# A two-layer decoder trunk on one core: the order of products around the chunk ends, side products placed later, and how zeros and stores are issued

## The chip, the core and the metric

One core of a Trainium2 chip runs the whole program in one launch. TensorE (PE in the profile) does the matrix products, VectorE (DVE), ScalarE (ACT) and GpSimd (POOL) the rest of the arithmetic, and SyncE (SP) issues almost all transfers between memory and the on-chip buffers. The metric is device microseconds of one execution, the median of several runs; less is better.

## The reference

512 tokens of width 1024, with 16 learned tokens put ahead of them, go through two layers. Each layer is a feed-forward half step, a token mixer and another feed-forward half step. Layer 0 mixes by chunked gated linear attention with 4 heads; layer 1 by sliding-window attention over one shared set of keys and values, which is made after layer 0. Each of the sub-layers has a norm ahead of it and one behind it. Cut to what matters:

```
def rmsnorm(x, g):
    return x * lax.rsqrt(jnp.mean(x * x, axis=-1, keepdims=True) + EPS) * g

def swiglu(x, w_in, w_out):
    gate, up = jnp.split(x @ w_in, 2, axis=-1)       # 1024 -> 2 x 2816
    return (jax.nn.silu(gate) * up) @ w_out          # 2816 -> 1024

h = jnp.concatenate([meta, x], axis=1)               # 16 + 512 tokens
for layer in range(2):
    g = norm_gains[layer]
    h = h + 0.5 * rmsnorm(swiglu(rmsnorm(h, g[0]), w_ffn_in[layer, 0], w_ffn_out[layer, 0]), g[1])
    hn = rmsnorm(h, g[2])
    mix = gla_mixer(hn, ...) if layer == 0 else swa_mixer(hn, ..., k_sh, v_sh)
    h = h + rmsnorm(mix, g[3])
    h = h + 0.5 * rmsnorm(swiglu(rmsnorm(h, g[4]), w_ffn_in[layer, 1], w_ffn_out[layer, 1]), g[5])
    if layer == 0:
        k_sh, v_sh = shared_kv(h, kv_norm, w_kv, cos, sin)
return h[:, 16:]
```

## The kernel before

**Layout.** Activations lie transposed: the width of 1024 is 8 tiles of 128 partitions, the tokens run along the free dimension. `H` is the residual stream, `Y` the output of a sub-layer before its norm. Tokens come in two groups, called gi 0 and gi 1: 272 and 256 in layer 0, 256 and 256 in layer 1 (the 16 added tokens are only needed as keys there). Every float32 operand is split into a high and a low half, each of the type fp32r: ACT copies the high half (L226, L245 for weights, L425 for inputs, L774 for hidden tiles), DVE subtracts to get the low half (L227, L246, L426, L775). A product is then three matmuls: high by high, low by high, high by low (`mm3s`, L333). All of them are issued by one helper, so nearly all have the line L162 in the profile, and are told apart by their tiles.

**A feed-forward block** (`ffn`, L604) goes over its 22 hidden tiles of 128 in four chunks of 4, 6, 6 and 6.

- The first chunk uses plain products. `x_first` (L509) computes several output tiles at once, in tiles named x, while the inputs of the norm are still being built one after another: all tiles for group 0, then all for group 1. A group of at most 256 tokens takes half a PSUM bank, so two outputs share one bank; each such bank is first written by a product of zeros, 512 wide (L532), and the products behind it only add. The same routine starts the two mixers and the shared keys and values (tiles x with inputs x_l0m, x_kv, x_l1m).
- The other chunks use seven products instead of eight for each 2 x 2 block (class `Strassen`, L711): `head`, `body` and `tail` issue the products 11, s1, s2, 12, s3, s4, 22 of 12 matmuls each into the banks a, c, d and e. ACT and DVE carry partial sums between the banks (L749 to L765). When the last product of a tile, "22" with the factor t4 in bank a, is done, a job called `gated` multiplies (L770, L771) and splits the hidden tile (L774, L775).
- After each chunk `out_proj` (L552) multiplies the chunk's hidden tiles by the output weights and adds the result into `Y` (tiles y). A *unit* is one output tile for one token group: three matmuls for each of the chunk's hidden tiles, the last hidden tile last. Layer 1 works 512 tokens wide there, but for the last chunk, which goes by the groups of 256.

**Norms.** Squares are added up on POOL and ACT (accumulators acc_...). A product with a matrix of ones (tiles st_...) sums over the partitions. `rstd` (L348) then computes an inverse square root with some eleven small instructions on POOL or DVE, puts it on a diagonal (dg_..., L383) and broadcasts it over the partitions by a second product (tiles r_...). `Operand.factors` (L436) does so ahead of a sub-layer, `Residual.run` (L453) behind one. The GLA mixer does it for each head (st_go, r_go).

**Order.** The order is made while the program is built. Side work is written as generators that give back a delay; `Flow` (L60) keeps a clock that moves on by an estimate for each matmul issued, and `flow.pump` between matmuls runs the jobs that are due. A wait of `flow.wait` runs jobs until the named ones are done, whatever the clock says. So the delays FACT (1.5), CHAIN (5) and STATE_KEYS (1.5) decide between which matmuls the st_, r_ and pk products stand. A scheduler then orders the instructions of each engine; an engine runs its own queue in order, and waits for other engines by semaphores.

**The end.** `Residual.store` (L471) scales `Y`, adds it to `H` and issues one transfer for each of the 8 tiles of 128 x 256 and each token group on SP, 16 in all (L482). For the second group the additions of tiles 0 to 3 are on POOL.

## Time and profile before

| | us |
|---|---|
| three runs | 1931.07, 1934.42, 1936.41 |
| median | 1934.42 |
| the profiled execution | 1931.38 |
| its span on the core | 1929.5 |

The mean granted clock of TensorE was 0.996 in the profiled execution. Rows of groups read: line, engine, operation, output tile and inputs, form, count; then busy time, mean ns of one, idle time of the engine just before them and what ended it. Rows of the timeline read: start, duration, engine, line, operation, output and inputs, form, count, and in brackets the idle time before and its releaser; a row with a count stands for several instructions in a row, and its duration runs to the end of the last.

### The profile page before, as it was taken

To read this page: it belongs to the slowest core of one execution; us is meant where nothing else is said; L and a number is where in the kernel's file an instruction comes from. 1 tells how busy PE (TensorE), PEld (TensorE's weight loads), DVE (VectorE), ACT (ScalarE), POOL (GpSimd) and SP (SyncE) were. 2 spreads that over 40 slices of the span, in tenths; PEclk is the share of its full clock that TensorE was granted. 3 is DMA by queue.
4 is the path that set the end of the run, shared out by engine and by line. 5 is a ranking of instruction groups with operands and counts; after the bars stand their busy time and mean duration, and the time that the engine had idled before them with its cause. 6 is when DMAs were issued, how large, how long until landed. Compare 5 with 4: busy or idle time off the path is not lost.

```text
span 1929.5 us, 37402 instructions
## 1 busy us (share of the span) xinstructions
PE 1888.9 (98%) x14522; PEld 1798.1 (93%) x14522; DVE 1420.1 (74%) x2868; ACT 1001.7 (52%) x2268; POOL 215.1 (11%) x417
## 2 busy tenths in 40 slices
PE   8999999999999999999999999999998999999997
PEld 7999999999999999999999898989976898989897
DVE  7885858676464788585887786868788779858584
ACT  5663636653245555353574453535645665636363
POOL 2000000321111400000033000000352140000002
PEclk9999999999999999999999999999999999999998
DMA  4332333322113123323351123233421212333331
GB/s 163 104 100 88 103 96 106 114 74 69 45 52 113 56 72 95 102 91 102 99 176 45 61 88 115 87 112 99 132 66 34 77 45 72 98 105 107 101 112 44
DMA packets 102144, 174.61 MB, mean 90 GB/s; under 512 B 11472, under 2 KB 24272, under 8 KB 101968
## 3 DMA queue, kind: packets, MB, share of 16 engines
q1 hardware_dynamic: 101680, 172.11, 28.2%
q8 instruction: 113, 1.85, 0.4%
q14 instruction: 63, 0.52, 0.1%
q10 hardware_dynamic: 288, 0.13, 0.0%
HBM read 170.10 MB, written 2.10 MB: 89 GB/s over the span
## 4 chain that ended last, share of the span: by engine, by line
PE 70%; DVE 19%; ACT 6%; issue 3%; POOL 1%; DMA 0%; SPq 0%; DVEq 0%; ACTq 0%; POOLq 0%
PE y L162 30%; PE x L162 16%; PE a L162 11%; DVE raw L251 5%; PE c L162 4%; DVE w_s L246 3%; DVE w L246 3%; ACT w_s L245 3%; PE d L162 2%; DVE w L227 2%; PE o L162 1%; ACT w L226 1%; PE po L162 1%; DVE hidl0f L775 1%; PE sc L162 0%
## 5 line engine op out<-in xcount | busy, mean ns | idle before, releaser
L246 DVE TENSOR_TENSOR w_s<-raw,w_s 128x512 fp32r<-128x512 f32 x288 | 194.0, 690 | 129.7 <-ACT w_s L245 127.6
L227 DVE TENSOR_TENSOR w<-raw,w 128x512 fp32r<-128x512 f32 x378 | 244.9, 673 | 31.1 <-ACT w L226 29.3
L162 PE MATMUL y<-hidl0f,w 128*128 128x256 f32 (+1 forms) x2112 | 261.0, 285 | 0.0
L162 PEld LDWEIGHTS y<-hidl0f,w 128*128 128x128 f32 x2112 | 258.8, 188 | 0.7
L245 ACT ACTIVATE w_s<-raw 128x512 fp32r<-128x512 f32 x288 | 175.3, 628 | 149.5 <-DVE raw L251 146.0
L162 PE MATMUL y<-hidl1f,w 128*128 128x512 f32 (+1 forms) x1344 | 249.8, 346 | 0.0
L162 PEld LDWEIGHTS y<-hidl1f,w 128*128 128x128 f32 x1344 | 212.0, 188 | 33.9 <-ACT hidl1f L774 0.4
L226 ACT ACTIVATE w<-raw 128x512 fp32r<-128x512 f32 x378 | 209.0, 586 | 46.0 <-PE y L162 39.4
L403 POOL TENSOR_TENSOR acc_post<-acc_post,sq_post 128x256 f32<-128x256 f32 (+1 forms) x72 | 56.9, 791 | 1386.5 <-ACT sq_post L402 1386.0
L251 DVE TENSOR_TENSOR raw<-raw,raw 128x512 f32<-128x512 f32 x288 | 198.0, 687 | 5.5
L246 DVE TENSOR_TENSOR w<-raw,w 128x512 fp32r<-128x512 f32 x216 | 148.3, 687 | 41.5 <-ACT w L245 40.2
L245 ACT ACTIVATE w<-raw 128x512 fp32r<-128x512 f32 x216 | 133.9, 621 | 48.0 <-PE y L162 47.7
L162 PE MATMUL x<-x_l0m,w 128*128 128x272 f32 (+1 forms) x1200 | 158.3, 288 | 0.0
L162 PEld LDWEIGHTS x<-x_l0m,w 128*128 128x128 f32 x1200 | 149.4, 189 | 1.2
L572 DVE TENSOR_TENSOR Y<-y,Y 128x256 f32<-128x256 f32 (+2 forms) x176 | 83.0, 473 | 74.4 <-PE y L162 73.8
L162 PE MATMUL a<-zl0f_t,w_s 128*128 128x264 f32 x864 | 117.8, 285 | 3.8 <-ACT c L751 3.8
L162 PE MATMUL a<-zl1f_t,w_s 128*128 128x256 f32 x864 | 115.1, 282 | 2.0 <-ACT c L751 1.6
L162 PEld LDWEIGHTS a<-zl0f_t,w_s 128*128 128x128 f32 x864 | 110.1, 188 | 5.0 <-ACT c L751 5.0
L162 PEld LDWEIGHTS a<-zl1f_t,w_s 128*128 128x128 f32 x864 | 106.9, 188 | 4.8 <-ACT c L751 4.8
L162 PE MATMUL x<-x_l0f,w 128*128 128x256 f32 (+1 forms) x768 | 100.0, 290 | 7.5 <-ACT w L226 5.8
L162 PEld LDWEIGHTS x<-x_l0f,w 128*128 128x128 f32 x768 | 96.6, 191 | 8.9 <-ACT w L226 5.8
L162 PE MATMUL x<-x_l1f,w 128*128 128x256 f32 (+1 forms) x576 | 93.1, 320 | 0.0
(485 smaller groups left out, 3306.5 us busy)
## 6 DMA issues: line engine op xcount, KB each, us to landing
raw<-in_w_in SPq DMA_DIRECT2D x352, 256.0 KB, 2.9
raw<-in_w_out SPq DMA_DIRECT2D x96, 256.0 KB, 3.3
raw<-in_gla_in SPq DMA_DIRECT2D x50, 256.0 KB, 3.0
raw<-in_w_last SPq DMA_DIRECT2D x48, 256.0 KB, 3.1
raw<-in_w_out SPq DMA_DIRECT2D x64, 128.0 KB, 3.0
raw<-in_gla_out SPq DMA_DIRECT2D x16, 256.0 KB, 2.9
raw<-in_w_q SPq DMA_DIRECT2D x16, 256.0 KB, 3.6
raw<-in_swa_out SPq DMA_DIRECT2D x16, 256.0 KB, 2.8
```

The costliest lines, as they stand in the source:

```text
L162: inst = pe.matmul(o, lhs, rhs, start=start, stop=stop, skip_group_check=onto)
L226: act.activation(w[:, 0, :m], raw[:, :m], AF.Copy)
L227: dve.tensor_tensor(w[:, 1, :m], raw[:, :m], w[:, 0, :m].bitcast(F32), op=ALU.subtract)
L245: act.activation(w[:, 0, :512], src, AF.Copy)
L246: dve.tensor_tensor(w[:, 1, :512], src, w[:, 0, :512].bitcast(F32), op=ALU.subtract)
L251: dve.tensor_tensor(dst, dst, src, op=ALU.add)
L403: pool.tensor_tensor(sums[0][:, :n], sums[0][:, :n], t[:, :n], op=ALU.add)
L572: dve.tensor_tensor(y, p[:, :n], y, op=ALU.add)
L775: dve.scalar_tensor_tensor(t.hid[:, 1, g], t.h, -1.0, t.hid[:, 0, g].bitcast(F32), op0=ALU.mult, op1=ALU.subtract)
```

## The change

There are four parts. (1) `out_proj` becomes a generator, `out_steps`, with a function `begin` that issues a unit's products but for the last hidden tile. In a chunk's last tile, `tail` issues the first unit's `begin` ahead of the product "22"; behind that product one more unit is begun where units are 512 tokens wide, two more else, and only then are the hidden tiles waited for. (2) `BEHIND` (1.5) is added to the delay of the norm factors of group 1, of the `STATE_KEYS` step of head 0, and of the r_go product of the last head. (3) `x_first` issues no products of zeros: the first product in a shared bank has the start flag, the second output in that bank has not. (4) `store` issues one transfer for two tiles; for the second token group those of tiles 2, 3 and 6, 7 are issued by ACT.

```diff
+BEHIND = 1.5
...
-        for o, w in outs:
-            mm(o, w[j // 4][:, 0, cols], xh, start and not shared, False)
-            mm(o, w[j // 4][:, 1, cols], xh, False, False)
         for i, (o, w) in enumerate(outs):
-            mm(o, w[j // 4][:, 0, cols], xl, False, stop and (not shared or i % 2 == 1))
+            second = shared and i % 2 == 1
+            mm(o, w[j // 4][:, 0, cols], xh, start and not second, False, second)
+            mm(o, w[j // 4][:, 1, cols], xh, False, False, second)
+        for i, (o, w) in enumerate(outs):
+            second = shared and i % 2 == 1
+            mm(o, w[j // 4][:, 0, cols], xl, False, stop, second)
             flow.pump()
...
-    def rstd(sq, n, dim, half, name, eng=pool):
+    def rstd(sq, n, dim, half, name, eng=pool, more=0.0):
...
-        yield DCHAIN if eng is dve else CHAIN
+        yield (DCHAIN if eng is dve else CHAIN) + more
...
-            nxt.rjob[gi] = flow.spawn(nxt.factors(gi))
+            nxt.rjob[gi] = flow.spawn(nxt.factors(gi), gi * BEHIND)
...
-                for j in (k, k + 1):
-                    sp.dma_start(out[j, :, o - META : o - META + n], H[:, j, o : o + n])
+                to = out[k : k + 2, :, o - META : o - META + n].rearrange("k p n -> p k n")
+                (act if gi and k % 4 else sp).dma_start(to, h)
...
                 banks = [ps(f"x{used[0]}_{i}_{gi}") for i in some[::2]]
-                for b in banks:
-                    mm(b.rearrange("p (a c) -> p a c", c=P), zeros, zeros.unsqueeze(1).to_broadcast([P, 4, P]), True, False)
...
-    def out_proj(hid, groups, split_groups, first, finish=None, tailm=0, packed=False):
+    def out_proj(*args, **named):
+        for _ in out_steps(*args, **named):
+            pass
+
+    def out_steps(hid, groups, split_groups, first, finish=None, tailm=0, packed=False, jobs=()):
...
+        begun = {}
+
+        def begin(m, g):
+            o, n = g
+            p = begun[m, o] = ps(f"y{used[0]}_{m}_{o}")
+            for j, t in enumerate(hid[:-1]):
+                w, c = tile_of(m, j)
+                mm3(p[:, :n], w, c, t, g, j == 0, False)
+
         def unit(m, g):
             o, n = g
-            p = ps(f"y{used[0]}_{m}_{o}")
-            for j, t in enumerate(hid):
-                w, c = tile_of(m, j)
-                mm3(p[:, :n], w, c, t, g, j == 0, j == nh - 1)
+            if (m, o) not in begun:
+                begin(m, g)
+            p = begun[m, o]
+            w, c = tile_of(m, nh - 1)
+            mm3(p[:, :n], w, c, hid[-1], g, nh == 1, True)
...
+        if jobs:
+            order = [(m, g) for m in range(KD - tailm) for g in groups]
+            order += [(m, split_groups[0]) for m in range(KD - tailm, KD)]
+            begin(*order[0])
+            yield
+            for m, g in order[1 : 2 if order[1][1][1] == SEQ else 3]:
+                begin(m, g)
+            flow.wait(*jobs)
...
-                    jobs.append(tiles.tail(cur, nxt is None))
+                    if nxt is None:
+                        fin = (finish, KD, True) if lo >= LAST else (None, 0, False)
+                        proj = out_steps(hids, groups, x.groups, False, *fin, jobs)
+                        end = used[0] + NLAST + tail
+                    jobs.append(tiles.tail(cur, proj if nxt is None else None))
                     cur = nxt
-            flow.wait(*jobs)
-            if lo < LAST:
-                out_proj(hids, groups, x.groups, ci == 0)
-            else:
+            if ci == 0:
+                flow.wait(*jobs)
+                out_proj(hids, groups, x.groups, True)
+                continue
+            if lo >= LAST:
                 set_ahead(32)
-                cap[0] = min(used[0] + NLAST + tail, len(units))
-                out_proj(hids, groups, x.groups, False, finish, KD, True)
+                cap[0] = min(end, len(units))
+            for _ in proj:
+                pass
...
-        def tail(self, t, last):
+        def tail(self, t, proj):
+            last = proj is not None
...
             act.activation(t.u2, t.u2, AF.Silu)
+            if last:
+                next(proj)
             self.product(t.a, t, "22", "t4", False)
...
-                yield STATE_KEYS
+                yield STATE_KEYS + (0 if h else BEHIND)
...
-                    r = yield from rstd(accs[gi], n, 256, True, f"go{h}_{gi}")
+                    r = yield from rstd(accs[gi], n, 256, True, f"go{h}_{gi}", more=h // 3 * BEHIND)
```

## The prediction

> **What bounds the kernel now.** I read the page first, then PE's waits, then PE's groups by line, the chain, and the timeline around each place that the diff touches.

> ```profile
> span 1929.5 us, 37402 instructions
> PE 1888.9 (98%) x14522; PEld 1798.1 (93%) x14522; DVE 1420.1 (74%) x2868; ACT 1001.7 (52%) x2268; POOL 215.1 (11%) x417
> PE   8999999999999999999999999999998999999997
> PEclk9999999999999999999999999999999999999998
> ```

> TensorE is busy in every slice at a full granted clock. Only three things can shorten this: fewer matmuls, fewer stalls of PE, or less time behind its last matmul. The view of PE's waits lists the stalls (microseconds in total, times, longest):

> ```profile
> PE x L162 <- ACT w L226: 5.8, 1, 5.8
> PE a L162 <- ACT c L751: 5.4, 12, 0.7
> PE r_post_out L162 <- DVE dg_post_out L383: 2.7, 1, 2.7
> PE sc L162 <- DVE pt L1157: 2.5, 1, 2.5
> PE sc L162 <- DVE Y L1117: 2.2, 2, 2.1
> PE r_go L162 <- POOL dg_go L383: 1.6, 1, 1.6
> PE sc L162 <- DVE q L1001: 1.3, 1, 1.3
> PE pk L174 <- DVE f L880: 1.3, 1, 1.3
> PE st_l1m L162 <- POOL acc_l1m L403: 1.1, 1, 1.1
> PE st_l0f L162 <- ACT acc_l0f L399: 1.1, 1, 1.1
> PE st_kv L162 <- POOL acc_kv L403: 0.7, 1, 0.7
> PE r_l0f L162 <- DVE dg_l0f L383: 0.6, 1, 0.6
> PE r_kv L162 <- POOL dg_kv L383: 0.2, 1, 0.2
> PE r_l0f L162 <- POOL dg_l0f L383: 0.2, 1, 0.2
> ```

> The first is the first weight's arrival, which the change does not touch. The others are short and scattered. The change aims at six named here: the r_, st_ and pk rows, except r_post_out.

> **Zeros.** Ten pairs of zero products go, each an instruction 512 wide. Their group, and one pair with what follows it on PE:

> ```profile
> L162 PE MATMUL x<-zeros 128*128 128x512 f32 x20 | 6.3, 395 | 0.0
> 23.32 0.64 PE L162 MATMUL x<-zeros 128*128 128x512 f32 x2
> 23.80 1.46 PE L162 MATMUL x<-x_l0f,w 128*128 128x256 f32 x11
> ```

> Matmuls overlap, so the mean of 395 ns overstates them: from the first zero to the next product 0.48 us pass for two, 0.24 each. The group's idle time is 0.0, so PE ran into them with work at hand. 10 x 0.48 = **-4.8 us**. The product that takes the start flag over costs no more than it did. [...]

> **Side products placed later.** The statistics products (st_) and the broadcast products (r_) of a second token group are fed by a chain on POOL, ACT or DVE; PE stands when it reaches them too early. BEHIND puts them 1.5 us of scheduler time later, about 12 of the 0.12 to 0.13 us products, and the idle times are 0.2 to 1.6 us, so a whole delay about covers each. What then fills the gap has to be ready itself, place by place:

> - Opening: r_l0f, 0.6. It stands behind 11 products of the second group now and behind 21 in the new order; ten more at 0.12 are 1.2 us, against 0.48 of zeros and 0.6 of idle taken away. **-0.6**.
> - r_go of the last head: 1.6. The new order puts 57 products between the statistics and it, about 7 us, and nothing new waits. **-1.6**.
> - Second FFN of layer 0: st_l0f 1.1 and r_l0f 0.2, filled by products whose inputs are built earlier. **-1.3**.
> - kv: st_kv 0.7 and r_kv 0.2. The filler needs the last kv input:

> ```profile
> 1035.61 0.38 PE L162 MATMUL st_kv<-ones,acc_kv 128*128 128x1 f32 x2 [0.68 <-POOL acc_kv L403]
> 1035.86 1.42 PE L162 MATMUL x<-x_kv,w 128*128 128x256 f32 x10
> 1037.28 0.48 DVE L426 SCALAR_TENSOR_TENSOR x_kv<-H,vec,x_kv 128x256 fp32r<-128x256 f32 x1
> ```

> PE is free at 1034.93 (1035.61 less 0.68). The 10 products take 1.2 and eight of the next run on the half that is ready (0.9), so it reaches the late half, ready at 1037.76, at about 1037.0: 0.7 of the 0.9 comes back. **-0.2**, between -0.9 and +0.2.
> - l1m: st_l1m 1.1, with the same trouble and more:

> ```profile
> 1418.22 0.38 PE L162 MATMUL st_l1m<-ones,acc_l1m 128*128 128x1 f32 x2 [1.13 <-POOL acc_l1m L403]
> 1418.46 1.54 PE L162 MATMUL x<-x_l1m,w 128*128 128x256 f32 x11
> 1419.28 0.67 DVE L426 SCALAR_TENSOR_TENSOR x_l1m<-H,vec,x_l1m 128x256 fp32r<-128x256 f32 x1 [0.58 <-ACT x_l1m L425]
> L227 DVE TENSOR_TENSOR w<-raw,w 128x512 fp32r<-128x512 f32 x378 | 244.9, 673 | 31.1 <-ACT w L226 29.3
> ```

> The last input is ready at 1419.95, and in the new DVE order one more weight split (0.67) is done before it: 1420.6. PE, free at 1417.09 and through statistics and 11 products about 1.8 later, at 1418.9, waits 1.7 there instead of 1.1: **+0.6**, between -1.1 (the input comes in time) and +1.3 (a second split is ahead of it).
> - pk: 1.3. Only five more products stand before it, 0.6 us, and the DVE instruction it waits for (f, L880) is itself queued behind more work in the new order. I take **0**, between -1.3 and +0.3.
> - l1f's second group shows no idle row, so the delay alone is worth **0**.

> **The attention of layer 1.** The l1m delay moves the broadcast that scales its queries: in the new order it stands behind a whole unit of query products, some 20 more of 0.12, 2.4 us. The sc rows (2.5, 2.2, 1.3) show that PE already waits there on a DVE/ACT chain. If all the lateness passes through, +2.4; if the query products now lie inside those waits, -2.4. Nothing in the trace leans either way: **0**.

> **Last product behind the first out-projection unit.** Is there a stall to win? The out-projection's groups, and one chunk end in time (L775 delivers the last hidden tile; the second row from below is one of the chain):

> ```profile
> L162 PE MATMUL y<-hidl0f,w 128*128 128x256 f32 (+1 forms) x2112 | 261.0, 285 | 0.0
> L162 PE MATMUL y<-hidl1f,w 128*128 128x512 f32 (+1 forms) x1344 | 249.8, 346 | 0.0
> 143.53 1.71 PE L162 MATMUL a<-zl0f_t,w_s 128*128 128x264 f32 x12 [0.56 <-ACT c L751]
> 145.93 1.62 PE L162 MATMUL a<-zl0f_t,w 128*128 128x264 f32 x12
> 148.97 0.71 DVE L775 SCALAR_TENSOR_TENSOR hidl0f<-c,hidl0f 128x528 fp32r<-128x528 f32 x1 [0.71 <-ACT hidl0f L774]
> 147.56 35.33 PE y L162 x288
> 343.68 2.54 PE L162 MATMUL y<-hidl0f,w 128*128 128x272 f32 x19
> ```

> The out-projection has 0.0 idle; 288 products run on from the last product without a gap, though the last tile is only ready at 149.68. So this part has nothing to remove: **0**. The 5.4 us of twelve a-waits on L751 are in the same place but before the moved product: the wait belongs to the product ahead of it (143.53), and its order with the ACT copy is unchanged. They stay. What it could lose: the last tile comes about 2.3 us behind the last product's last matmul (147.4 to 149.68). In the new order 30 products of 0.13 (19 took 2.54), 3.8 us, stand between, in the wide groups 15 of about 0.23, 3.5 us. In a last chunk DVE does four weight splits (0.67 each) first, so there 2.3 + 2.7 = 5.0 is the worst. I take 0, up to +0.5 in each of the four last chunks.

> **Stores.** The end of the kernel:

> ```profile
> 1921.08 2.49 DVE L479 TENSOR_TENSOR t_out<-Y,r_post_out 128x512 f32<-128x512 f32 x4 [1.45 <-PE r_post_out L162]
> 1923.14 4.00 SPq L482 DMA_DIRECT2D out<-H  x8
> 1923.48 1.28 DVE L480 TENSOR_TENSOR H<-t_out,H 128x512 f32<-128x512 f32 x2
> L482 SPq DMA_DIRECT2D out<-H x16: 332/410/446, 1906.1 to 1926.7; - x16
> DMA to landing us min/median/max: 1.7/1.8/1.9
> raw<-in_w_in SPq DMA_DIRECT2D x352, 256.0 KB, 2.9
> ```

> The data is done at 1924.76 (1923.48 + 1.28), but SP issues eight transfers of 0.41 us one by one, the last at 1926.7. Four transfers of pairs on two queues follow the data: the last is issued at about 1924.8, a gain of 1.9. A pair is 256 KB; its landing is not shown, and lies between 1.8 (128 KB out) and 2.9 (256 KB in). Gain between 0.8 and 1.9; nearest is the store row plus some growth, so **-1.2**. ACT issues two of them; nothing is queued behind them on ACT. [...]

> **Sum.** -4.8 zeros, -0.6 opening, -1.6 r_go, -1.3 l0f, -0.2 kv, +0.6 l1m, -1.2 stores, the rest 0: **-9.1 us**. The profiled execution took 1931.38 us (span 1929.5), so 1922.3. The runs' median, 1934.42, is 3.0 above it: 1925.3, told as **1925**. With the lower ends (pk -1.3, l1m -1.7 below its value, kv -0.7, attention -2.4, stores -0.7) it is 6.8 less, 1918.5; with the upper ones (pk 0.3, l1m 0.7, kv 0.4, attention 2.4, stores 0.4, four late tiles 2.0) 6.2 more, 1931.5; all at once is unlikely, so its own range is 1919 to 1930.

> **Rivals.** A change under 0.3% (5.8 us) can't be told from none here.

> - *Also the dependent waits go* (chance 0.15): pk and the attention's waits are covered by the query and weight products that now lie in them, the inputs come in time. For it: these are waits of a queue's order, not of a full engine (DVE 74%). Against it: DVE's own order puts more before L880. -9.1 - 1.3 - 2.4 - 1.7 = -14.5, about 1920.
> - *Side delays give back what they remove* (0.22): every st_ and r_ wait turns up again as a wait on the input build behind it, as I expect for l1m; only zeros and stores remain. For it: the kv and l1m builds above. Against it: l0f and r_go have far earlier inputs. -4.8 - 1.2 = -6.0, 1928.4. In half of this the attention takes 2.4 too, 1931.
> - *The last tile becomes a wait at every chunk end* (0.12, the slower side). The new order fixes when PE asks for the last hidden tile; before, matmuls of several units stood between. If DVE and ACT put weight splits before L770 to L775 everywhere, the tile is 2.3 + 4 x 0.67 = 5.0 us late against 3.5 to 3.8 of cover: 1.2 to 1.5 at twelve places, +14 to +18. It decides from 0.76 at each (9.1 / 12). 1934.4 - 9.1 + 16 = 1941. Against it: in the chunk end shown, L775 waits on ACT's hidl0f alone (0.71 idle), with no split ahead of it.
> - *The reorder does what it is said to and also removes the L751 waits* (0.03): -5.4 more, 1920. The order of those instructions doesn't support it.

> **How the numbers follow.** Forecast 0.48, the rivals 0.15, 0.22, 0.12 and 0.03. Below 1928.6 (faster by over 0.3%): the forecast but for 0.05, the two larger gains, and half of the give-back: 0.43 + 0.18 + 0.11 = 0.72. Same: 0.05 + 0.11 = 0.16. Slower: 0.12. The range reaches from the larger gains to the give-back with a late attention: 1918 to 1932; left out are the slower rival and some 0.06 below.

> **What would show it.** Right: the zeros' group is gone; the waits of r_go, st_l0f, st_kv and both r_l0f are gone; a wait of PE x on DVE or ACT x_l1m of 1 to 2 us is new; a<-L751 still holds about 5 us in 12; the y groups stay at 0.0 idle; out<-H is x8 of 256 KB with a landing near 2.4, its last issue right behind the last addition. Wrong: y waits on L774 or L775 at chunk ends, the three sc waits above their present 6.0 us together, pk's wait above 1.6, or the L751 waits gone.

## The result, and the profile after

| | us |
|---|---|
| changed kernel, median of 9 runs | 1938.97 (1938.05 to 1943.20) |
| kernel before, median of 9 runs beside it | 1935.23 |
| ratio | 1.0023, 95% interval [1.0014, 1.0032] |
| profiled execution of the changed kernel | 1943.20, span 1941.3 |

The change made the kernel slower by 0.23%, where 0.5% faster was forecast (the ratio is the one on record; the quotient of the two medians is 1.0019). That is less than the 0.3% set as the bound of "no change", but its interval is clear of 1. Both profiled executions lie at an end of their kernel's runs: the one of before ran at a mean granted clock of 0.996, the 80 runs of before beside the experiments at 0.991 to 0.995; the one of the changed kernel at 0.990, its other eight runs at 0.991 or 0.992. So the two profiles are 11.8 us apart, the medians 3.7.

Page of the changed kernel (span; then busy time and instructions by engine):

```profile
span 1941.3 us, 37347 instructions
PE 1897.9 (98%) x14502; PEld 1806.3 (93%) x14502; DVE 1419.3 (73%) x2868; ACT 1000.7 (52%) x2268; POOL 225.0 (12%) x417
```

PE has 20 instructions less, and is busy for 9 us longer. POOL has the same 417 instructions and is busy for 10 us longer. Neither engine was given more to do: the same instructions took longer. The changed kernel's view of PE's waits:

```profile
PE r_go L163 <- POOL dg_go L387: 6.2, 3, 2.3
PE a L163 <- ACT c L782: 5.8, 12, 1.0
PE ptm L175 <- DVE mt L1169: 5.7, 3, 2.6
PE r_post_out L163 <- DVE dg_post_out L387: 2.6, 1, 2.6
PE sc L163 <- DVE Y L1151: 1.3, 1, 1.3
PE x L163 <- ACT x_l1m L429: 1.3, 1, 1.3
PE r_kv L163 <- POOL dg_kv L387: 0.3, 1, 0.3
PE x L163 <- DVE x_kv L430: 0.3, 1, 0.3
PE pk L175 <- DVE f L914: 0.2, 1, 0.2
```

The waits that the change aimed at are gone (both st_ rows of l0f and l1m, st_kv, r_l0f) or small. In their place r_go waits at three heads that had no wait at all, and ptm, a transpose in the attention, waits three times, where before the score products (sc) waited. The twelve waits on the ACT copy into c are as they were (5.8 against 5.4), and the out-projection still has no idle time (groups of the changed kernel, last field):

```profile
L163 PE MATMUL y<-hidl0f,w 128*128 128x272 f32 (+1 forms) x2112 | 260.9, 285 | 0.0
L163 PE MATMUL y<-hidl1f,w 128*128 128x512 f32 (+1 forms) x1344 | 249.7, 346 | 0.0
```

**Where the time went.** The starts of certain products on PE cut both executions into the same stages. The last column is the best kernel of the experiments, run e5 below. Differences from before's profiled execution, us:

| stage | forecast | changed | e5 |
|---|---|---|---|
| opening and first chunk | -1.1 | -1.6 | -2.2 |
| rest of the first block | 0 | -0.3 | -0.3 |
| l0m and the four GLA heads | -2.1 | +7.6 | -2.1 |
| GLA output projection to the chunks of the next block | -1.8 | -2.0 | -2.1 |
| rest of that block | 0 | +0.1 | +0.1 |
| kv | -1.6 | -1.4 | -1.4 |
| first block of layer 1, to l1m's statistics | -0.5 | -0.6 | -0.8 |
| l1m and the attention | +0.1 | +11.5 | +5.1 |
| l1f | -1.0 | -1.1 | -1.1 |
| last block | 0 | +0.3 | +0.1 |
| end | -1.2 | -0.7 | -0.8 |

In the changed kernel nine of the eleven stages came out within 0.5 us of the forecast. Between these two executions, all of the loss is in two.

**First place: the GLA heads.** One head's norm in the kernel before, by the timelines of POOL, DVE and PE:

```profile
456.51 0.20 POOL L369 TENSOR_TENSOR wv_go<-wv_go,zv_go 68x4 f32<-68x4 f32 x1
457.06 0.23 POOL L376 TENSOR_SCALAR wv_go<-wv_go 68x4 f32<-68x4 f32 x1
459.52 0.78 DVE L816 TENSOR_TENSOR qk<-x,R_l0m 128x272 f32<-128x272 f32 x2 [6.98 <-PE x L162]
460.23 1.45 DVE L852 TENSOR_TENSOR_SCAN b<-resets,ls 128x528 f32<-128x528 f32 x1
460.06 1.26 PE L162 MATMUL r_go<-dg_go,ones 68*128 68x272 f32 x4
```

and in the changed kernel:

```profile
457.48 0.65 POOL L373 TENSOR_TENSOR wv_go<-wv_go,zv_go 68x4 f32<-68x4 f32 x1
458.21 1.01 POOL L372 TENSOR_SCALAR wv_go<-zv_go 128x2 f32<-128x2 f32 x1
459.30 1.11 POOL L380 TENSOR_SCALAR wv_go<-wv_go 68x4 f32<-68x4 f32 x1
456.79 1.29 DVE L228 TENSOR_TENSOR w<-raw,w 128x512 fp32r<-128x512 f32 x2
457.99 1.25 DVE L886 TENSOR_TENSOR_SCAN b<-resets,ls 128x528 f32<-128x528 f32 x1
459.16 1.23 DVE L887 TENSOR_TENSOR_SCAN b<-resets,ls 128x528 f32<-128x528 f32 x1
462.89 2.03 PE L163 MATMUL r_go<-dg_go,ones 68*128 68x272 f32 x4 [2.10 <-POOL dg_go L387]
```

In the rows shown, POOL's small instructions took 0.2 us while DVE stood idle, and 0.65 to 1.11 while DVE ran weight splits and scans: each ends about when a DVE instruction ends. 42 products stand between the statistics and r_go in both kernels; the chain got longer under them. Delays early in the stage had brought DVE's work into the time of POOL's chain.

**Second place: the clock.** The changed kernel in slices of 2 us right behind that wait (the third number from the right is the granted clock):

```profile
460.00:462.00 2.00, 0.79 (x7) 0.58 (x5) 0.39 (x1) 0.21 (x1) 1.92 (x11) 1.00 0.18 69
462.00:464.00 2.00, 0.99 (x3) 0.56 (x4) 0.34 (x1) 0.00 (x0) 1.60 (x5) 0.95 0.00 0
464.00:466.00 2.00, 2.00 (x8) 1.72 (x8) 1.42 (x4) 0.19 (x1) 0.00 (x0) 0.50 0.00 0
466.00:468.00 2.00, 2.00 (x15) 2.00 (x14) 0.57 (x3) 1.90 (x4) 0.00 (x0) 0.69 0.00 0
468.00:470.00 2.00, 2.00 (x19) 1.96 (x18) 2.00 (x6) 1.93 (x4) 0.00 (x0) 1.00 0.00 0
```

Behind the stall PE runs at half clock for about 3.4 us: 8 products in 2 us in place of 19. So this wait of 2.1 us is paid with 1.7 more. The same holds at the second head (2.26 us); behind the third wait (1.87) the clock stays at 1.00. In the stage, PE's waits sum to 6.5 us against 2.8 before, and 6.8 us are at half clock against none: 3.6 and 3.4 of the 7.6 us. In the attention the half clock lasts longer:

```profile
1415.00:1430.00 15.00, 13.46 (x74) 11.99 (x73) 9.44 (x19) 5.59 (x13) 9.38 (x20) 0.77 0.36 105
1460.00:1475.00 15.00, 15.00 (x83) 10.80 (x85) 10.82 (x35) 8.30 (x37) 1.06 (x1) 0.64 0.13 37
```

Added up over slices of 0.5 us in the GLA, kv and attention stages, one minus the clock makes 15.4 us in this execution, and 1.7 in before's.

The loss in the attention belongs mostly to the execution that was profiled, and not to the new order. Four kernels of the experiments (e1, e5, e6, e8; their runs follow below) have the instructions of the changed kernel in exactly its order on PE, DVE, ACT and POOL from the first product on x_l1m on; two others (e9, e10) have before's order there. From that product to the statistics behind the attention (st_post_l1f), in the one profile of each:

| kernel | at half clock, us | stage, us |
|---|---|---|
| changed | 23.9 | 165.7 |
| e8 | 23.9 | 165.5 |
| e6 | 17.1 | 163.3 |
| e5 | 10.2 | 159.3 |
| e1 | 6.8 | 157.5 |
| before | 3.4 | 154.2 |
| e9, e10 (order of before) | 10.2 | 157.2, 157.1 |

With one and the same order the stage takes from 157.5 to 165.7 us, about half a microsecond more for each at half clock. With half of that time taken off, the changed kernel and before are 1.3 us apart here, as much as PE's waits in that stage (10.1 us against 8.8). Nor are the runs as a whole as far apart as the two profiles. One minus the mean clock, times the span, is an estimate of what the clock cost a run (the record has the clock to three places): on average 13.5 us in the 80 runs of before, 16.6 in the nine of the changed kernel and 10.0 in the five of e5. So of the 4 us between an average run of before and of the changed kernel, some 3 are clock.

### The profile page after: what moved, and what is told of

Same layout as the page of the kernel before. It is cut to its first block, busy times and chain, and to the rows that moved or that the text cites. A ratio compares the mean times of both kernels' runs of the same rounds, so it can differ in the third digit from the quotient of the medians.

```text
span 1941.3 us, 37347 instructions
## 1 busy us (share of the span) xinstructions
PE 1897.9 (98%) x14502; PEld 1806.3 (93%) x14502; DVE 1419.3 (73%) x2868; ACT 1000.7 (52%) x2268; POOL 225.0 (12%) x417
## 2 busy tenths in 40 slices
PE   8999999999999999999999999999998999999997
## 4 chain that ended last, share of the span: by engine, by line
PE 72%; DVE 18%; ACT 5%; issue 3%; POOL 2%; DMA 0%; SPq 0%; DVEq 0%; ACTq 0%; POOLq 0%
PE y L163 30%; PE x L163 16%; PE a L163 12%; DVE raw L252 4%; PE c L163 4%; DVE w_s L247 3%; DVE w L247 3%; ACT w_s L246 3%; PE d L163 3%; DVE w L228 1%; PE o L163 1%; PE po L163 1%; ACT w L227 1%; DVE hidl0f L809 1%; PE sc L163 0%
## 5 line engine op out<-in xcount | busy, mean ns | idle before, releaser
L163 PE MATMUL y<-hidl0f,w 128*128 128x272 f32 (+1 forms) x2112 | 260.9, 285 | 0.0
L227 ACT ACTIVATE w<-raw 128x512 fp32r<-128x512 f32 x378 | 207.9, 586 | 33.4 <-PE y L163 29.3
## 6 DMA issues: line engine op xcount, KB each, us to landing
raw<-in_w_in SPq DMA_DIRECT2D x352, 256.0 KB, 2.9
raw<-in_w_out SPq DMA_DIRECT2D x96, 256.0 KB, 3.3
raw<-in_gla_in SPq DMA_DIRECT2D x50, 256.0 KB, 3.1
raw<-in_w_last SPq DMA_DIRECT2D x48, 256.0 KB, 3.1
raw<-in_gla_out SPq DMA_DIRECT2D x16, 256.0 KB, 2.7
raw<-in_w_q SPq DMA_DIRECT2D x16, 256.0 KB, 3.9
raw<-in_swa_out SPq DMA_DIRECT2D x16, 256.0 KB, 2.9
```

The lines of the kernel that those rows point to most:

```text
L163: inst = pe.matmul(o, lhs, rhs, start=start, stop=stop, skip_group_check=onto)
L227: act.activation(w[:, 0, :m], raw[:, :m], AF.Copy)
```

## The experiments

Every kernel ran beside the kernel before on the same chip, in three sets: e1, e2, e3 and e0; e4 to e7; e8 to e11. Ratios are to the kernel before of the same set. The changed kernel ran in none of these sets, so a difference from its 1938.97 goes across sets; the medians of before lie between 1935.23 and 1935.93.

### Taking early delays back

```diff
-                yield STATE_KEYS + (0 if h else BEHIND)
+                yield STATE_KEYS
```

> The changed kernel with the delay of the STATE_KEYS step of head 0 taken back (1.5 us less there), all else as changed. Theory A (the delay shifts the phase of all four GLA heads, so that DVE's weight splits and scans run beside GpSimd's chain for r_go and stretch it): the three r_go waits (6.2 us in the changed kernel) fall below 1 us, the granted clock in the GLA stage is 1.00 throughout, and the time falls by 7 to 9 us, to about 1930. Rival B (the phase is set by the later l0m factors or by the missing zeros, not by this delay): r_go waits stay near 6 us and the time within 2 us of 1939.

Run e1: 1935.13 (1930.24 to 1937.10), ratio 0.9990 [0.9981, 0.9999]: 3.8 less than the changed kernel, half of what was expected. r_go still waited 4.9 us, now at all four heads, though none for longer than 1.6; the clock in the GLA stage was 1.00. The waits as a whole did not shrink, as pk waits 1.7 us again (4.9 + 1.7 against 6.2 + 0.2): what the stage won, 3.8 us, is about what 6.8 us at half clock had cost. So this delay was one cause, and not the only one.

```diff
-            nxt.rjob[gi] = flow.spawn(nxt.factors(gi), gi * BEHIND)
+            nxt.rjob[gi] = flow.spawn(nxt.factors(gi), 0 if nxt.name == "l1m" else gi * BEHIND)
```

> The changed kernel with the delay of l1m's second group of norm factors taken back, all else as changed. Theory A (the later broadcast of l1m's factors starts the attention late and empties PE long enough for the clock to be granted at half): the half clock of 1422 to 1430 is gone, the stage from r_l1m to the end of the attention is as long as before (r_l1m to r_post_l1f 128 us, against 133 in the changed kernel), and the time falls by 4 to 8 us. Rival B (the loss in the attention comes from the other changes): the time stays within 2 us of 1939.

Run e2: 1940.33, ratio 1.0023 [1.0014, 1.0032]: no gain, theory A fell. Without the delay st_l1m waits for 3.1 us instead, and the half clock behind that wait was there all the same, from 1422 to 1429.

> The changed kernel with both of these delays taken back. If both theories hold and the two places don't depend on each other, the gains add: 12 to 16 us less than the changed kernel, 1924 to 1927, which is what was forecast for the change (1925). If one place gives back what the other wins, about 1931.

Run e3: 1934.99, ratio 0.9994 [0.9985, 1.0003]: about what the first of the two gave alone, so the gains did not add.

```diff
-BEHIND = 1.5
+BEHIND = 0.0
```

> The changed kernel with every added delay set to 0 (BEHIND = 0): only the reordered chunk ends, no zeros and paired stores are left. By the terms of the forecast, zeros -4.8 and stores -1.2 and no side product moved: about 1929. If the missing zeros alone shift the phase of the GLA heads, r_go waits of heads 0 to 2 are there too and the time is 1935 or more.

Run e0: 1936.29, ratio 0.9997 [0.9988, 1.0006], neither of the two. r_go waited only at the last head (1.6), as before, so the missing zeros don't shift the heads. But the zeros' gain was missing too.

### The other early delay, and the best kernel

```diff
-                yield STATE_KEYS + (0 if h else BEHIND)
+                yield STATE_KEYS
...
-            nxt.rjob[gi] = flow.spawn(nxt.factors(gi), gi * BEHIND)
+            nxt.rjob[gi] = flow.spawn(nxt.factors(gi), 0 if nxt.name in ("l0m", "l1m") else gi * BEHIND)
```

> The changed kernel with the delays of head 0's STATE_KEYS step, of l0m's factors and of l1m's factors taken back; those of l0f1, kv, l1f1 and of the last head's r_go stay. Theory A (either early delay, l0m's or STATE_KEYS', shifts the phase of the four GLA heads against the query and key products, and then DVE instructions with two inputs in the on-chip buffer stretch GpSimd's small instructions in the r_go chain): the r_go waits fall to 0 to 0.5 us (4.9 with l0m's delay alone, 1.6 with none), the GLA stage from pk of head 0 to the output projection is 2 us shorter than before's 154.5, the clock there is 1.00, and the time is 1928 to 1931 against 1935 of the kernel before. Rival B (what moves the phase is the missing zeros or the reordered chunk ends): r_go waits stay above 3 us, 1934 or more.

Run e4: 1930.14, ratio 0.9972 [0.9962, 0.9983], r_go 0.4 us in all, as expected. The next kernel is the same with `("l0m",)` for the names:

> As the run before it, but l1m's delay stays. If the l1m delay removes st_l1m's wait and with it the half clock of the following stretch, 2 to 4 us less than the run before it. If the attention's own chain on ACT and DVE sets the end of that stage, and the half clock falls by chance of the window, within 2 us of it.

Run e5: **1926.12** (1923.67 to 1929.85, five runs), ratio 0.9955 [0.9943, 0.9968]: 9.8 us faster than the kernel before and 12.9 faster than the change as made. It is 4.0 less than e4, the first of the two outcomes: st_l1m's wait of 3.1 us is gone, and the attention was at half clock for 10.2 us in its profile against 20.5 in e4's. Its GLA stage in one slice, beside that of the changed kernel (first e5, then the changed kernel; the last (x25) belongs to POOL, and the clock follows):

```profile
430.00:470.00 40.00, 38.75 (x315) 36.85 (x314) 23.72 (x51) 14.91 (x33) 5.09 (x25) 1.00 0.24 78
```

```profile
430.00:470.00 40.00, 37.55 (x289) 35.22 (x289) 21.62 (x46) 13.10 (x30) 7.64 (x25) 0.96 0.21 67
```

The same 25 POOL instructions take 5.09 and 7.64 us. With l0m's delay kept back and the other one in:

> The changed kernel with l0m's delay alone taken back; the delay of head 0's STATE_KEYS step and all others stay. It tells which of the two early delays shifts the phase of the GLA heads: with l0m's alone (an earlier run) the r_go waits were 4.9 us, with neither 0.4. Theory A (either of them shifts the phase): r_go waits of 3 us or more, GpSimd above 5.5 us busy in 40 in the chains of heads 0 to 2, time above 1930. Rival B (only l0m's delay matters, the keys' delay is harmless by itself): r_go waits near 0.4 and 1925 to 1928.

Run e8: 1933.97, ratio 0.9991 [0.9982, 1.0000]; r_go waited 3.4 us at three heads, and POOL was busy for 7.1 us in 40 in the chains of the first two heads. So each early delay does it: r_go's waits are 0.4 with neither, 3.4 and 4.9 with one, 6.2 with both.

### Is the chain late, or PE early?

```diff
-                    r = yield from rstd(accs[gi], n, 256, True, f"go{h}_{gi}", more=h // 3 * BEHIND)
+                    r = yield from rstd(accs[gi], n, 256, True, f"go{h}_{gi}", more=BEHIND)
```

> The changed kernel with r_go of all four heads placed 1.5 us later, not of the last alone; the order before it is as changed. Theory A (the chain is stretched, PE comes to it too early): GpSimd stays as busy in the chains as in the changed kernel (about 7.6 us in 40, against 5.1 before), and the waits of heads 0 to 2 fall from 2.1 to 2.3 us each to below 1, with the clock there back at 1.00: 4 to 8 us less than the changed kernel, 1931 to 1935. Rival B (GpSimd's chain is late for another reason, such as work queued ahead of it): the waits stay at 2 us each, and the time at 1939.

Run e6: 1929.75, ratio 0.9968 [0.9958, 0.9978], 9.2 below the changed kernel, more than expected. POOL's chain is stretched as in the changed kernel, but 57 products now cover it:

```profile
430.00:470.00 40.00, 39.39 (x317) 37.22 (x317) 23.43 (x49) 13.82 (x32) 7.64 (x25) 1.00 0.25 80
```

POOL 7.64 again in the first head's slice, PE 39.39 busy at clock 1.00, r_go 0.6 in all. The stretch costs nothing where the cover is longer than it.

### What a stall costs

In the kernel before, r_go of heads 0 to 2 is moved ahead by shortening the delay by 1.5 (30 products of cover instead of 42) and by 3.0 (15 products):

```diff
-        yield DCHAIN if eng is dve else CHAIN
+        yield (DCHAIN if eng is dve else CHAIN) - less
...
-                    r = yield from rstd(accs[gi], n, 256, True, f"go{h}_{gi}")
+                    r = yield from rstd(accs[gi], n, 256, True, f"go{h}_{gi}", less=0.0 if h == 3 else 3.0)
```

> The kernel before with r_go of heads 0 to 2 moved earlier by hand: 30 products behind the statistics instead of 42, nothing else changed. It measures what a stall of a known size costs. 12 products of 0.125 are 1.5 us, less some 0.3 of slack: waits of about 1.1 us at three places, 3.4 us in all. Theory (a stall costs itself, and the clock is granted at half for some microseconds behind it only where PE stood for over about 2 us): clock 1.00 in the GLA stage, 3 to 4 us over the kernel before. Rival (short stalls bring the half clock too): 5 us or more, half clock behind the waits. Rival (the stall costs nothing, since the products behind it wait anyway): within 1.5 us.

Run e9: 1939.74, ratio 1.0021 [1.0012, 1.0030]: 4.0 more. r_go waited 4.8 in all (1.6 before), and the clock behind the three moved ones stayed at 1.00: the stalls, 1.0 to 1.1 us each and 3.2 in all, cost themselves. The theory's bound of 2 us did not hold, though: in the same profile the last head's r_go, which was not moved, waits for 1.25 us, and half clock follows it for 3.4 us, from 570.4 on.

> The same with 15 products instead of 42: 27 x 0.125 = 3.4 us earlier, waits of about 3.0 us at three places, 9 us in all. Theory (a stall above some 2 us also costs the half clock behind it): half clock for 3 to 7 us behind each of the three waits, 1.5 to 3.5 us lost at each, so 13 to 19 us over the kernel before. Rival (the half clock comes by chance or from other things, not from the stall): clock 1.00 in the GLA stage, 8 to 10 us over the kernel before.

Run e10: 1948.01, ratio 1.0064 [1.0050, 1.0077]: 12.3 more, just under the expected range. r_go waited 9.6, 8.0 more than before, so 4.3 us are something else. What else changed there is the clock, which is at half behind each of the three waits, for 13.7 us in all in the profile. The first of them, 2.85 us long, ends at 459.36:

```profile
458.00:460.00 2.00, 0.64 (x2) 0.30 (x2) 0.00 (x0) 0.00 (x0) 1.86 (x7) 0.98 0.00 0
460.00:462.00 2.00, 1.92 (x8) 1.51 (x7) 1.19 (x2) 0.00 (x0) 0.15 (x1) 0.50 0.00 0
462.00:464.00 2.00, 2.00 (x14) 2.00 (x13) 0.74 (x2) 1.66 (x3) 0.00 (x0) 0.67 0.00 0
464.00:466.00 2.00, 2.00 (x19) 1.97 (x18) 1.09 (x3) 1.59 (x3) 0.00 (x0) 1.00 0.00 0
```

### Parts of the change alone

The kernel before with the reordered chunk ends (`out_steps`, `begin`, `tail` as in the change) and nothing else:

> The kernel before with the reordered chunk ends alone (first part of the change): nothing else changed. Theory A (there was no stall to remove, the out-projection had 0.0 idle): a within 0.5 us in 12 of the waits on L751, y idle 0.0, time within 1.5 us of the kernel before. Rival C (the new order removes or adds a wait at each of the twelve chunk ends): 4 us or more to either side.

Run e7: 1934.76, ratio 0.9992 [0.9983, 1.0001]; waits on L751's copy 5.5 in 12. This part does nothing that can be measured.

The kernel before with the new `mm3s` and without the products of zeros (L532), nothing else:

> The kernel before without the products of zeros (third part of the change alone): nothing else changed. The forecast priced it at -4.8 us. Theory (the zeros stood ahead of side products that wait for GpSimd, so where they go the waits of st_kv, r_kv, st_l1m and r_l1f grow, st_l1m's to about 3 us with half clock behind it): 0 to 2 us less than the kernel before. Rival (the forecast's step is right and the loss came from elsewhere): 4 to 5 us less.

Run e11: 1937.57, ratio 1.0009 [1.0000, 1.0018]: 20 matmuls less, and no gain; slower, if anything. The waits of that kernel:

```profile
PE st_l1m L162 <- POOL acc_l1m L406: 3.1, 1, 3.1
PE st_kv L162 <- POOL acc_kv L406: 1.1, 1, 1.1
PE r_kv L162 <- POOL dg_kv L386: 1.0, 1, 1.0
PE r_l1f L162 <- POOL dg_l1f L386: 0.8, 1, 0.8
```

Before, these were 1.1, 0.7, 0.2 and none: 4.0 us more waits for 4.8 us less work, and the half clock from 1420 to 1426.7 behind the longest. The zeros had been cover. st_l1m's wait grew by more (2.0) than the two pairs of zeros ahead of it (1.0); in that kernel POOL does two more rope instructions, 2.0 us, ahead of the sum that st_l1m waits for.

## Why the prediction was wrong, point by point

- **What bounds the kernel.** "TensorE is busy in every slice at a full granted clock" was true of the one profiled execution, and was taken for a constant. The other runs of before have a lower mean clock, and what a stall does to the clock was put at nothing without a reason. This step failed; by the estimate above it is worth some 3 us between average runs. (A slip beside it: the rows that the change aims at are eight, of seven tiles, not six.)
- **Side products placed later.** At the places that it named, the step held: l0f, kv, l1f and the last r_go came within 0.3 us of their terms. It failed in its list of places, and this is the step that turned the gain into a loss: it costed a delay only where PE waited already. l0m's delay has no entry in it, the keys' delay is there for pk's own wait alone, and "nothing new waits" was said of the last head's r_go without looking at the heads that had no wait. l0m's delay and the keys' delay shift DVE's work of all heads against POOL's chains; heads 0 to 2 then wait for 6.2 us and, twice, run at half clock behind it: +7.6 in that stage against -2.1 forecast. With these two delays left out the stage is worth -2.1 (e5), and the whole kernel takes 12.9 us less than the changed one, where the forecast had missed by 12.8 (3.7 against -9.1).
- **pk.** Priced at 0; its wait fell from 1.3 to 0.2 in the changed kernel, by the keys' delay (it was 0.3 with that alone in e8, 1.7 with l0m's alone in e1), one of the two that cost the heads so much.
- **Zeros.** Rightly counted (0.24 us each), wrongly priced. "PE ran into them with work at hand" is no proof that the time is won, as the next stop behind them was a wait. Alone they are worth nothing (e11), and with no delay nothing (e0); with the delays that cover those waits they may be worth a part of e5's 9.8, which no run measures apart. Two terms of the sum were not independent.
- **l1m and the attention.** The forecast wait on x_l1m came (1.3 plus 0.2 on its two halves). The 0 for the attention, with bounds of 2.4, is out by 11.5 us for l1m and the attention between the two profiles, but not in its waits, which are 1.3 us longer: some 10 of the 11.5 us are half clock (20.5 us more of it; the ptm wait of 2.6 is followed by the clock of 0.64), for which the forecast had no term. e1 has the same order there and a clock of 1.00 from 1415 to 1430 in its profile: the same order runs at either clock. e1's runs spread with it, from 1930.24 us at a mean clock of 0.996 to 1937.10 at 0.993.
- **Last product.** Priced at 0, measured at 0 (e7). The slower rival had put its loss there; the loss came elsewhere, by a mechanism that no rival had. Of the signs that the forecast named, only one told of it: r_go's wait was not gone. None of the signs of being wrong appeared (y idle 0.0, the sc waits 2.2 us together, pk 0.2, the L751 waits 5.8 in 12): they watched the places that had been costed.
- **Stores.** The end is 0.7 us shorter instead of 1.2. ACT's second store is issued as the last addition ends (1937.2), but the stores land later than assumed:

```profile
L486 SPq DMA_DIRECT2D out<-H x6: 372/373/399, 1918.5 to 1936.6; - x6
L486 ACTq DMA_DIRECT2D out<-H x2: 403/450/496, 1936.8 to 1937.2; - x2
DMA to landing us min/median/max: 2.1/2.2/3.0
out<-H ACTq DMA_DIRECT2D x2, 256.0 KB, 2.9
```

A pair lands after 2.2 us from SP and 2.9 from ACT, where a single store took 1.8; 2.4 was taken for all.

The size forecast (-9.1 us) is about what the change is worth without two of its delays: e5 has -9.8. Some of that match is luck, as by the estimate above 3.5 us of e5's gain are clock (13.5 against 10.0), which the forecast did not count. Why the attention falls to half clock in one execution and not in another with the same instructions is taken up in the last section.

## What to carry to other kernels

Where a stall is filled, or filler is taken out, ask what all the engines do at that time: a delay of one side product shifts every later one, and can lay one engine's work over another's chain at places that have no wait today (here 6.2 us of r_go at three heads). A stall on TensorE can cost 1.7 us or more beyond its length, half of the 3.4 us or more at half clock behind it: here from about 1.3 us on, counted from one start on PE to the next, it did so at times, above 3 us in all three cases. Whether it does differs from one execution to the next (6.8 to 23.9 us at half clock in the attention with one and the same order), so one profile does not tell. Cheap filler ahead of a stall may be earning its time (e11: 4.8 us of zeros less, 4.0 us of waits more). Change such delays one by one, and look at the busy time of an unchanged count of instructions: POOL's 5.1 against 7.6 us for the same 25 was the first sign.

## What the runs showed of the hardware

**GpSimd's small instructions beside VectorE's.** Over the profiles of before, the changed kernel and the first four experiments, 652 of POOL's small instructions (68x4 and 128x2) have no DVE instruction beside them: median 0.193 us, longest 0.228. 69 that lie for more than half of their time under a weight split (w<-raw,w) have a median of 0.52, 18 under a scan of 1.14. Under DVE instructions with one operand in PSUM (qk<-x,R_l0m) it is 0.19, as without any. The splits and the scans have no operand in PSUM; that this, and not another difference between these instructions, makes POOL's longer is the author's reading, which no run tests by itself.

```profile
1485.29 1.30 PE L162 MATMUL sc<-kz,q 64*128 64x272 f32 x8 [2.55 <-DVE pt L1157]
1485.00:1488.00 3.00, 2.71 (x33) 2.36 (x35) 3.00 (x12) 1.87 (x6) 0.00 (x0) 1.00 0.00 0
```

```profile
1491.55 2.00 PE L162 MATMUL sc<-kz,q 64*128 64x272 f32 x8 [2.55 <-DVE pt L1157]
1492.00:1495.00 3.00, 3.00 (x20) 2.29 (x18) 3.00 (x10) 1.87 (x6) 0.00 (x0) 0.50 0.00 0
```

So stalls of 1.3 to 2.6 us were enough at times. What decides between 0.9 and 1.8 us of a window stays open.
